# The opening of a diffusion layer kernel: modulation computed in four quarters instead of two halves

## The chip, the cores and the metric

The kernel runs on one core of one Trainium2 chip. The metric is the device time of one execution in microseconds (us). All arithmetic is in float32; large matrix products split each operand into a rounded part and a remainder and take three TensorE products.

## The reference, cut to what matters

One layer: adaLN-modulated RMSNorm, one wide input projection, two branches (attention and a gated MLP), an output projection, then a second modulated norm and an MLP. The change touches only what comes first:

```python
mod_x = jax.nn.silu(c) @ w_mod[l] + b_mod[l]            # c: 1024 values; w_mod: 1024 x 6144
sh1, sc1, g1, sh2, sc2, g2 = jnp.split(mod_x[:, None, :], N_MOD, axis=-1)
mod_c = jax.nn.silu(c_ctx) @ w_mod[l] + b_mod[l]        # the same for the context's vector
...
h_x = modulate(x, norm1_g[l], sh1, sc1)                 # rmsnorm(x, g) * (1 + scale) + shift
p_x = h_x @ w_in[l]                                     # x: 2048 tokens x 1024; w_in: 1024 x 3840
```

So the first projection needs the first two sixths of `w_mod` (shift and scale, 1024 columns each, 8 MB together) times two vectors, plus the first rows of `x`.

## The kernel before, in words

**Projection.** `project` treats 1024 tokens at a time as two blocks of 512 (`x0` and `x1` in the opening), and 1024 input channels as two halves of 512. Over this 2 x 2 split it uses a seven-product scheme: products 0, 1, 5, 6, 4, 2, 3 in this order (`SUMS`) replace eight. Product 0 needs only `x0`'s first 512 channels, product 1 only its second 512. Product 5 is the first that needs `x1`, through two differences per 128 channels (`h_five`). Each product runs in two chunks of 24 matmuls (`pairs_run`: four token tiles, two rows of 128 channels, three matmuls for the split operand, lines 1744 to 1746). Between chunks, and in the middle of one, `hook` runs a step of the generator `opening`.

**Operands.** `turn` transposes a 128-channel column of four token tiles on TensorE (line 192) and lets ScalarE apply scale and shift (line 537, from `G1` and `S1`). `operand` casts the result on ScalarE (line 572) and takes the remainder on VectorE (line 573). `pair_chunk` does the same for a weight chunk (lines 712, 713), and `opening_terms` builds weight differences for product 5 and on (lines 621 to 633; tiles `hx`, `f`). `leave` copies product 1's results out and `take` puts product 0's back (lines 2125, 727).

**Modulation.** `mod_head` loads `c`, `c_ctx`, `b_mod`, `norm1_g` and the spatial bias with five small transfers, loads `x0` and the weights for the first 512 channels (16 tiles of 128 x 512 from two places of `w_mod`), multiplies them (`mod_products`, line 339: 16 matmuls of 512 columns, 32 passes), and `mod_finish` turns the row into columns of `S1` and `G1` (lines 348 to 361). Then product 0 can start. The second half of the weights is loaded behind `x1`, and its 16 matmuls stand in `opening` after product 0. `h_scale` squares `x` on ScalarE (line 515), takes an inverse root on VectorE and multiplies `x` by it (line 524).

**Order.** The opening's instructions are pinned: each engine runs them in the order in which the code is written. All loads go through SyncE's queue in the written order. `at` in `pairs_run` sets how many weight chunks are prepared ahead.

Of the kernel before, what the change touches and what calls it, by code (L numbers as in the profile page):

```python
# [18 lines left out]
P = 128  # L19
# [48 lines left out]
CONTEXT_AT = 20  # L68
ON_VECTOR = (2, 4, 8, 14)
# [3 lines left out]
class Kern:  # L73
# [207 lines left out]
    def mod_head(self):  # L281
# [4 lines left out]
        at = 0  # L286
        for src, eng in (
            (I["c"][0], nc.sync),
            (I["c_ctx"], nc.sync),
            (I["b_mod"][0, : 2 * D], nc.scalar),  # L290
            (I["norm1_g"][0], nc.scalar),
        ):
            src = src.rearrange("(k p) -> k p", p=P)
            eng.dma_start(rows[at : at + src.shape[0]], src)
            at += src.shape[0]
        nc.scalar.dma_start(rows[at : at + GROUPS], I["gm_bs"][0])
        self.rope_consts()
        at += GROUPS
# [20 lines left out]
        w = self.mod_weights(0, "hx")  # L319
        self.h_scale(self.x0, dve=True)  # L320
        ps = self.bank([TB])
        for k in range(KC):
            self.mod_products(ps, w, k)
        self.mod_finish(ps, 0)

    def mod_weights(self, half, tag):
        w = []
        for k in range(KC):
            w.append([self.sb(tag, [TB]) for _ in range(2)])
            for i, t in enumerate(w[k]):  # L330
                lo = i * D + half * TB
                self.nc.sync.dma_start(
                    t, self.I["w_mod"][0, k * P : (k + 1) * P, lo : lo + TB]
                )
        return w

    def mod_products(self, ps, w, k):
        for i in range(2):
            self.nc.tensor.matmul(
                ps[32 * i : 32 * i + 32], self.wide[:, k, :], w[k][i],  # L340
                start=k == 0, stop=k == KC - 1,
            )

    def mod_finish(self, ps, half):
        nc = self.nc
        bcol, gcol = self.mod_cols
        row = self.t2([TB])
        nc.scalar.copy(row[:64], ps[:64])
        pt = self.bank([HK, 64])
        for j in range(HK):  # L350
            nc.tensor.transpose(
                pt[:, j, :], row[:64, j * P : (j + 1) * P], self.ident[:64, :64]
            )
        ks = slice(half * HK, (half + 1) * HK)
        for i, dst in enumerate((self.S1, self.G1)):
            bs = slice(i * KC + half * HK, i * KC + (half + 1) * HK)
            nc.vector.tensor_tensor(
                out=dst[:, ks], in0=pt[:, :, 32 * i : 32 * i + 2],
                in1=bcol[:, bs].unsqueeze(2).broadcast_to([P, HK, 2]), op=ALU.add,
            )  # L360
        nc.vector.scalar_tensor_tensor(
            out=self.G1[:, ks], in0=self.G1[:, ks], scalar=1.0,
            in1=gcol[:, ks].unsqueeze(2).broadcast_to([P, HK, 2]),
            op0=ALU.add, op1=ALU.mult,
        )
# [350 lines left out]
    def pairs_run(self, pairs, h, ready, hook, direct):  # L716
# [395 lines left out]
    def project(self, tail):  # L1112
# [4 lines left out]
        loaded = [self.pair_load(pairs[0], 0, c) for c in range(2)]  # L1117
        x1 = self.x_load(self.x_block(1), TT, lambda n: self.sb("hx", n), 2)
        wm = self.mod_weights(1, "h")
        loaded += [self.pair_load(pairs[0], 1, c) for c in range(2)]  # L1120
# [5 lines left out]
        h[0], h[1] = [], []  # L1126
        at = self.here()
        for kk in range(HK):
            t = raw[0, kk] = self.m4([2, TB])
            self.turn(self.x0, kk, t[:, 0])  # L1130
            if kk % 2 == 0:
                ready.append(self.pair_chunk(pairs[0], 0, kk // 2, loaded[kk // 2]))
            h[0].append(self.operand(0, t[:, 0]))
        self.h_scale(x1, dve=True)

        def opening(raw=raw, h=h):
            for _ in range(4):
                yield
            ps = self.bank([TB])
            for k in range(KC):  # L1140
                self.mod_products(ps, wm, k)
            self.mod_finish(ps, 1)
            for c in range(2):
                for kk in (2 * c, 2 * c + 1):
                    t = raw[0, kk]
                    self.turn(self.x0, kk + HK, t[:, 1])
                    h[1].append(self.operand(1, t[:, 1]))
                ready.append(self.pair_chunk(pairs[0], 1, c, loaded[2 + c]))
                next(terms)
# [13 lines left out]
            self.h_five(raw, h, 2)  # L1163
            next(terms)
            self.h_five(raw, h, 3)
            yield
            self.pins.append(range(at, self.here()))
            self.fences.append(range(at, self.here()))
            next(terms)
            yield  # L1170
            for _ in range(3):
                yield
                next(terms, None)
            for _ in range(CONTEXT_AT - 13):
                yield
# [1217 lines left out]
def kernel(ctx: ExitStack, tc: tile.TileContext, ins: dict, out: bass.AP):  # L2393
# [4 lines left out]
    "x", "c", "ctx", "c_ctx", "w_mod", "b_mod", "norm1_g", "norm2_g", "w_in", "q_norm_g",  # L2398
    "k_norm_g", "gm_norm_g", "gm_ws", "gm_bs", "w_br_attn", "w_br_gm", "w_out", "w_ff1",
# [35 lines left out]
```

## Time and profile before

| | |
|---|---|
| three runs | median 3011.93 us (3010.1 to 3013.86) |
| profiled execution | 3006.42 us, its span 3004.3 us |
| granted TensorE clock | 0.992 of full speed, mean |
| busy: TensorE / VectorE / ScalarE / GpSimd | 97% / 69% / 47% / 22% |
| VectorE busy in the span's first 116 us | 72.44 us |

The span runs from the first to the last instruction; the execution's own time is some 2 us longer. A row of the timeline gives start, duration, engine, line of the code, operation, output and inputs, shapes, and in brackets how long the engine sat idle before it and what ended that. "Windows" give the busy time of each engine in a stretch, then the granted clock (1.00 is full), the busy share of the DMA engines and what they moved.

### The profile page before, as it was taken

The numbers are of one execution on the slowest core, as the hardware profiler recorded it, in microseconds if no ns is written. First come the engines' busy times: TensorE is split into PE (matmuls) and PEld (weight loads), VectorE is DVE, ScalarE is ACT, GpSimd is POOL, SyncE is SP. The second block draws the span as 40 slices with busy tenths as digits, with TensorE's granted clock in tenths as the row PEclk, the third lists the DMA queues.
The fourth block names the chain that finished last, engine by engine and source line by source line (L and its number), as shares of the span: only waits on it lengthen the run. The fifth ranks groups of instructions, "written<-read, shape, count | busy, mean of one in ns | idle before, by whom it ended". The sixth has DMA issues, their size and how long they took to land.

```text
span 3004.3 us, 37936 instructions
## 1 busy us (share of the span) xinstructions
PE 2929.0 (97%) x13325; PEld 2211.2 (74%) x13325; DVE 2073.7 (69%) x2983; ACT 1418.8 (47%) x2318; POOL 654.0 (22%) x470
## 2 busy tenths in 40 slices
PE   7899999999999999999999989999999999999999
PEld 5778788876555555556888878888887888888887
DVE  4857487766888898777555588776676766654555
ACT  5645765554454454544222354444454344444432
POOL 0000000001999899894121200000000000000000
PEclk9999999999999999999999999999999999999999
DMA  7687966775010010016776659888766544447654
GB/s 269 190 288 258 313 211 215 255 250 163 24 36 29 22 37 22 22 43 193 232 218 188 189 194 320 306 302 306 262 218 221 182 152 155 154 164 267 210 210 154
DMA packets 386175, 559.04 MB, mean 186 GB/s; under 512 B 38640, under 2 KB 192416, under 8 KB 385984
## 3 DMA queue, kind: packets, MB, share of 16 engines
q1 hardware_dynamic: 373616, 535.89, 53.7%
q10 hardware_dynamic: 12368, 20.73, 1.8%
q8 instruction: 105, 1.72, 0.2%
q14 instruction: 86, 0.70, 0.1%
HBM read 379.75 MB, written 176.69 MB: 185 GB/s over the span
## 4 chain that ended last, share of the span: by engine, by line
PE 82%; DMA 7%; DVE 7%; ACT 2%; issue 2%; SPq 0%; POOL 0%; DVEq 0%; ACTq 0%; POOLq 0%
PE b L1744 14%; PE b L1745 14%; PE b L1746 14%; PE b L2322 9%; PE b L2291 5%; PE b L2310 4%; PE b L186 4%; PE b L187 4%; PE b L188 4%; PE b L2246 3%; PE a L1744 2%; PE a L1745 2%; PE a L1746 2%; PE b L192 1%; DMA m<-ws_d 1%
## 5 line engine op out<-in xcount | busy, mean ns | idle before, releaser
L2257 DVE TENSOR_REDUCE ts<-b 128x1 f32<-128x512 f32 x492 | 301.8, 681 | 66.9 <-PE b L2246 66.9
L2342 POOL TENSOR_TENSOR ac<-ac,p 128x512 f32<-128x512 f32 x214 | 313.6, 1498 | 48.3 <-ACT p L2314 48.3
L1860 DVE TENSOR_TENSOR b<-b,b 128x1024 fp32r<-128x1024 f32 x170 | 200.7, 1220 | 136.5 <-ACT b L1859 136.1
L1859 ACT CAST b<-b 128x1024 fp32r<-128x1024 f32 x170 | 170.7, 1051 | 226.1 <-PE b L1746 100.1
L2314 ACT ACTIVATE p<-b 128x512 f32<-128x512 f32 x384 | 193.8, 627 | 168.3 <-PE b L2310 160.6
L1745 PE MATMUL b<-b,b 128*128 128x512 f32 x680 | 265.1, 390 | 3.5 <-DVE b L1860 3.5
L1744 PE MATMUL b<-b,b 128*128 128x512 f32 x680 | 266.2, 391 | 2.3 <-DVE f L1881 1.4
L1746 PE MATMUL b<-b,b 128*128 128x512 f32 x680 | 264.7, 389 | 0.0
L2342 POOL TENSOR_TENSOR ac<-p,p 128x512 f32<-128x512 f32 x32 | 52.8, 1667 | 742.1 <-ACT p L2314 742.1
L2342 POOL TENSOR_TENSOR ac<-ac,t 128x512 f32<-128x512 f32 x152 | 198.9, 1337 | 0.0
L2291 PE MATMUL b<-h,h 128*128 128x512 f32 x576 | 187.0, 405 | 3.3 <-ACT p L2314 2.0
L2322 PE MATMUL b<-p,h 128*64 128x512 f32 x768 | 186.9, 610 | 0.0
L2310 PE MATMUL b<-h,h 128*128 128x512 f32 x576 | 178.6, 391 | 0.0
L1745 PE MATMUL b<-hb,b 128*128 128x512 f32 x446 | 173.8, 390 | 0.0
L1754 DVE TENSOR_TENSOR f<-f,b 128x512 f32<-128x512 f32 x160 | 109.1, 682 | 82.5 <-issue 47.8
L1744 PE MATMUL b<-hb,b 128*128 128x512 f32 x415 | 161.8, 390 | 0.0
L1746 PE MATMUL b<-hb,b 128*128 128x512 f32 x415 | 161.3, 389 | 0.0
L1745 PEld LDWEIGHTS b<-b,b 128*128 128x128 f32 x680 | 127.6, 188 | 31.7 <-DVE b L1860 5.0
L2291 PEld LDWEIGHTS b<-h,h 128*128 128x128 f32 x576 | 103.6, 188 | 63.9 <-DVE ts L2257 24.3
L1744 PEld LDWEIGHTS b<-b,b 128*128 128x128 f32 x680 | 127.7, 188 | 30.7 <-ACT b L1859 3.4
L1746 PEld LDWEIGHTS b<-b,b 128*128 128x128 f32 x680 | 127.6, 188 | 26.3
L1757 ACT ACTIVATE f<-f 128x512 f32<-128x512 f32 x96 | 60.5, 630 | 141.7 <-DVE f L1754 141.7
(440 smaller groups left out, 7260.8 us busy)
## 6 DMA issues: line engine op xcount, KB each, us to landing
ao_d<-f SPq DMA_DIRECT2D x224, 256.0 KB
f<-in_w_ff SPq DMA_DIRECT2D x48, 1024.0 KB
b<-ao_d SPq DMA_DIRECT2D x85, 512.0 KB
b<-w2o_d SPq DMA_DIRECT2D x85, 512.0 KB
w2o_d<-f SPq DMA_DIRECT2D x112, 256.0 KB
f<-in_w_in SPq DMA_DIRECT2D x38, 512.0 KB
f<-x_d SPq DMA_DIRECT2D x64, 256.0 KB
hb<-ao_d SPq DMA_DIRECT2D x54, 256.0 KB
```

Source lines behind the costliest of these rows:

```text
L186: mm(ps, sh, mh, start=start, stop=False)
L1744: mm(ps, wh, hh, start=start and k == 0, stop=False, skip_group_check=True)
L1745: mm(ps, wh, hl, start=False, stop=False, skip_group_check=True)
L1746: mm(ps, wl, hh, start=False, stop=k == len(w) - 1, skip_group_check=True)
L1859: nc.scalar.copy(h, f32(l))
L1860: nc.vector.tensor_tensor(out=l, in0=f32(l), in1=f32(h), op=ALU.subtract)
L2257: nc.vector.tensor_reduce(out=self.mx[:, t, h, c : c + 1], in_=ps[h], axis=AX.X, op=ALU.max)
L2291: self.nc.tensor.matmul(self.pts[j][h], k.KA[c][self.kv][:, ks], self.qa[h], start=True, stop=False, skip_group_check=True,)
L2310: self.nc.tensor.matmul(s, k.KB[c][self.kv][:, ks], self.qb[h], start=False, stop=True, skip_group_check=True,)
L2314: self.nc.scalar.activation(pt[h], s, AF.Exp)
L2322: nc.tensor.matmul(self.o[h * HD : (h + 1) * HD, :], k.V[c][:, i, self.kv * HD : (self.kv + 1) * HD], pt[h], start=j == 0, stop=j == NKT - 1,)
L2342: nc.gpsimd.tensor_tensor(out=self.acc[e][:, h], in0=old[:, h], in1=pt[h], op=ALU.add)
```

## The change

The weights of the modulation are laid out anew in HBM: `w_mod1[q, k]` holds, for quarter `q` (256 channels) and row block `k`, shift and scale columns side by side, so one transfer of 128 x 512 brings both. The five small vectors are concatenated to `head`, one transfer. The modulation runs in four quarters: quarter 0 in front of everything, quarters 1 to 3 in steps of `opening`. The row product of quarter 1 stands in the middle of product 0's first chunk, that of quarter 2 in the middle of its second; that of quarter 3 stands behind the whole first chunk of product 1. Each `quarter` prepares the operands of one chunk. `x1` is loaded behind the third quarter's weights, and it is scaled after quarter 2. The steps that turn `x1` and form product 5's operands come one or two steps later.

```diff
+MQ = 2
...
-        for src, eng in (
-            (I["c"][0], nc.sync),
-            (I["c_ctx"], nc.sync),
-            (I["b_mod"][0, : 2 * D], nc.scalar),
-            (I["norm1_g"][0], nc.scalar),
-        ):
...
+        at = I["head"].shape[0]
+        nc.sync.dma_start(rows[:at], I["head"])
         self.rope_consts()
...
+    def mod_weights(self, q, tag):
         w = []
         for k in range(KC):
+            t = self.sb(tag, [2, MQ * P])
+            self.nc.sync.dma_start(t.rearrange("p i c -> p (i c)"), self.I["w_mod1"][q, k])
+            w.append(t)
+        return w
+
+    def mod_row(self, w):
+        nc = self.nc
+        ps = self.bank([MQ * P])
+        for k in range(KC):
+            for i in range(2):
+                nc.tensor.matmul(
+                    ps[32 * i : 32 * i + 32], self.wide[:, k, :], w[k][:, i],
+                    start=k == 0, stop=k == KC - 1,
                 )
+        row = self.t2([MQ * P])
+        nc.scalar.copy(row[:64], ps[:64])
+        return row
...
-            depth = 3 if direct is None else min(3, max(1, at - 2))
+            depth = 3 if direct is None or at > 5 else 1
...
+        wm, loaded = [], []
+        for q in range(4):
+            if q == 3:
+                x1 = self.x_load(self.x_block(1), TT, lambda n: self.sb("hx", n), 2)
+            wm.append(self.mod_weights(q, "h" if q > 1 else "hx"))
+            loaded.append(self.pair_load(pairs[0], q // 2, q % 2))
...
+        def quarter(q, raw=raw, h=h):
+            j, c = q // 2, q % 2
+            for kk in (2 * c, 2 * c + 1):
+                if not j:
+                    raw[0, kk] = self.m4([2, TB])
+                t = raw[0, kk][:, j]
+                self.turn(self.x0, kk + j * HK, t)
+                if kk == 2 * c:
+                    ready.append(self.pair_chunk(pairs[0], j, c, loaded[q]))
+                h[j].append(self.operand(j, t))
+
+        quarter(0)
 
         def opening(raw=raw, h=h):
-            for _ in range(4):
-                yield
...
+            yield
+            row = self.mod_row(wm[1])
+            yield
+            self.mod_finish(row, 1)
+            quarter(1)
+            yield
+            row = self.mod_row(wm[2])
+            yield
+            self.mod_finish(row, 2)
+            quarter(2)
+            self.h_scale(x1, dve=True)
+            yield
+            yield
+            self.mod_finish(self.mod_row(wm[3]), 3)
+            quarter(3)
+            next(terms)
             yield
             turned = self.raw_turned(1, x1, raw, self.t4)
             next(turned)
             next(terms)
             yield
             next(turned)
+            next(terms)
             self.h_five(raw, h, 0)
+            self.h_five(raw, h, 1)
             yield
             next(turned)
-            self.h_five(raw, h, 1)
             next(terms)
+            self.h_five(raw, h, 2)
...
```

Line numbers move with the edit: line 537 becomes 524, 572 becomes 559, 524 becomes 511, 515 becomes 502, 348 becomes 330, 631 becomes 618, 2125 becomes 2124, 727 becomes 714, 1744 to 1746 become 1743 to 1745.

What the order of instructions shows, first on TensorE at product 0. Before, its four token tiles (`a_694` to `a_697`) run through and the second half of the modulation stands behind the whole product:

```order
L1746 MATMUL a_696<-f_99_634,h_649 128x384
L1744 MATMUL a_697<-f_99_634,h_637 128x384
L1745 MATMUL a_697<-f_43_515,h_637 128x384
L1746 MATMUL a_697<-f_99_634,h_638 128x384
L1744 MATMUL a_697<-f_99_634,h_648 128x384
L1745 MATMUL a_697<-f_43_515,h_648 128x384
L1746 MATMUL a_697<-f_99_634,h_649 128x384
L339 MATMUL b_754<-h_532,t_5_406 32x512
L339 MATMUL b_754<-h_533,t_5_406 32x512
```

After, on TensorE between the two pairs of token tiles of product 0's first chunk (`a_621` to `a_624`):

```order
L1745 MATMUL a_622<-f_90_603,h_618 128x384
L325 MATMUL b_637<-hx_466,t_5_402 32x256 x2
L325 MATMUL b_637<-hx_468,t_5_402 32x256 x2
L325 MATMUL b_637<-hx_470,t_5_402 32x256 x2
L325 MATMUL b_637<-hx_472,t_5_402 32x256 x2
L325 MATMUL b_637<-hx_474,t_5_402 32x256 x2
L325 MATMUL b_637<-hx_476,t_5_402 32x256 x2
L325 MATMUL b_637<-hx_478,t_5_402 32x256 x2
L325 MATMUL b_637<-hx_480,t_5_402 32x256 x2
L1743 MATMUL a_623<-f_90_603,h_606 128x384
```

A quarter's 16 matmuls of 256 columns moved into the chunk; the transposes of the next quarter follow the chunk.

Second, VectorE ahead of quarter 3 (`hx_516`, `hx_517` are parts of `x1`, `S_74` and `G_73` are `S1` and `G1`), after the change:

```order
L511 TENSOR_SCALAR hx_513<-hx_513,ts_798 128x512
L511 TENSOR_SCALAR hx_516<-hx_516,ts_798 128x512
L511 TENSOR_SCALAR hx_517<-hx_517,ts_798 128x512
L344 TENSOR_TENSOR S_74<-b_864,ts_405 128x4
L344 TENSOR_TENSOR G_73<-b_864,ts_405 128x4
L348 SCALAR_TENSOR_TENSOR G_73<-G_73,ts_406 128x4
L700 TENSOR_TENSOR f_68_538<-f_67_536,f_144_876 128x768
```

The scaling of `x1` stands ahead of quarter 3's columns; before, it stood ahead of the second half's.

Third, ScalarE from product 1's leaves to product 5's operands. Before (`t_148`, `t_153`: `x1` turned; `f_151`: product 5's weights; `h_894`: its first operand; `t_159`: a leave):

```order
L537 ACTIVATE t_148_847<-b_848,S_74,G_73 128x512
L537 ACTIVATE t_148_847<-b_854,S_74,G_73 128x512
L631 CAST f_151_860<-hx_806 128x384
L631 CAST f_151_860<-hx_833 128x384
L537 ACTIVATE t_153_878<-b_879,S_74,G_73 128x512
L537 ACTIVATE t_153_878<-b_885,S_74,G_73 128x512
L572 CAST h_894<-t_156_891 128x512
L2125 COPY t_159_904<-a_694 128x384
L2129 DMA p_d_0_129<-t_159_904 128x384
```

After (`t_161`: the second turned tile of `x1`; `t_160`: the last leave; `f_164`: product 5's weights; `h_976`, `h_983`: its first two operands):

```order
L2124 COPY t_160_950<-a_624 128x384
L2128 DMA p_d_0_129<-t_160_950 128x384
L714 COPY a_624<-t_116_702 128x384
L524 ACTIVATE t_161_954<-b_955,S_74,G_73 128x512
L524 ACTIVATE t_161_954<-b_961,S_74,G_73 128x512
L618 CAST f_164_967<-hx_895 128x384
L618 CAST f_164_967<-hx_932 128x384
L559 CAST h_976<-t_166_973 128x512
L559 CAST h_983<-t_169_980 128x512
```

The weights' cast and the first operands moved behind all four leaves of product 1 and behind the second turned tile. On VectorE at the same place, after the change:

```order
L620 TENSOR_TENSOR f_165_968<-hx_895,f_164_967 128x384
L620 TENSOR_TENSOR f_165_968<-hx_932,f_164_967 128x384
L570 TENSOR_TENSOR m_596<-m_596,t_154_917 128x512
L571 TENSOR_TENSOR t_166_973<-t_154_917,m_596 128x512
L560 TENSOR_TENSOR h_977<-t_166_973,h_976 128x512
L570 TENSOR_TENSOR m_610<-m_610,t_161_954 128x512
```

The remainder of the weights (line 620) stands ahead of the first operand's differences (570, 571), as before; the second operand's differences stand behind the first's remainder.

More of the change, by code (lines that the diff above doesn't have):

```diff
@@ L318, in mod_head, with mod_finish @@
         self.x0 = self.x_load(self.x_block(0), TT, self.t4)
-        w = self.mod_weights(0, "hx")
         self.h_scale(self.x0, dve=True)
[L321 to L326, printed above, removed]
+    def mod_weights(self, q, tag):
         w = []
         for k in range(KC):
[L329 to L333, printed above, removed]
-                )
[L335 to L344, printed above, removed]
+            t = self.sb(tag, [2, MQ * P])
[10 more added lines that the diff above has]
+                    start=k == 0, stop=k == KC - 1,
+                )
+        row = self.t2([MQ * P])
+        nc.scalar.copy(row[:64], ps[:64])
+        return row
+    def mod_finish(self, row, q):
         nc = self.nc
         bcol, gcol = self.mod_cols
[L347 to L350, printed above, removed]
+        pt = self.bank([MQ, 64])
+        for j in range(MQ):
             nc.tensor.transpose(
@@ L1116, in project @@
         at = self.here()
[L1117 to L1120, printed above, removed]
+        wm, loaded = [], []
[4 more added lines that the diff above has]
+            loaded.append(self.pair_load(pairs[0], q // 2, q % 2))
         raw, h = {}, [None] * 7
@@ L1126, in project @@
         h[0], h[1] = [], []
+        row = self.mod_row(wm[0])
+        self.mod_finish(row, 0)
         at = self.here()
[L1128 to L1134, printed above, removed]
-        def opening(raw=raw, h=h):
-            for _ in range(4):
-                yield
[L1139 to L1149, printed above, removed]
+        def quarter(q, raw=raw, h=h):
[9 more added lines that the diff above has]
+        quarter(0)
+        def opening(raw=raw, h=h):
+            yield
[14 more added lines that the diff above has]
+            next(terms)
             yield
```

32 lines of the change are left out of this document (15 added, 17 removed).

## The prediction

> **What bounds the kernel now.** The page comes first:
>
> ```profile
> span 3004.3 us, 37936 instructions
> PE 2929.0 (97%) x13325; PEld 2211.2 (74%) x13325; DVE 2073.7 (69%) x2983; ACT 1418.8 (47%) x2318; POOL 654.0 (22%) x470
> PE   7899999999999999999999989999999999999999
> ```
>
> TensorE is the bound; it idles 75 us of the span, and the first slice (75 us) is the emptiest. The change touches only this opening. So the question is how much later or earlier TensorE gets through it; behind it TensorE is nearly full, and a shift is carried to the end. The opening as the timeline has it (start, duration, engine, line):
>
> ```profile
> 11.87 11.12 PE L339 MATMUL b<-hx,t 128*32 128x512 f32 x32 [6.25 <-DMA hx<-in_w_mod]
> 23.02 0.58 ACT L348 COPY t<-b 64x512 f32<-64x512 f32 x1 [10.78 <-PE b L339]
> 23.66 0.46 PE L351 MATMUL b<-ident,t 64*128 64x64 f32 x4 [0.67 <-ACT t L348]
> 24.74 0.78 ACT L537 ACTIVATE m<-b,S,G 128x512 f32<-128x512 f32 x1 [1.14 <-PE b L192]
> 26.81 0.45 PE L1744 MATMUL a<-f,h 128*128 128x384 f32 x1 [0.80 <-ACT h L572]
> 27.47 0.62 ACT L572 CAST h<-m 128x512 fp32r<-128x512 f32 x1
> 31.27 0.52 PE L1744 MATMUL a<-f,h 128*128 128x384 f32 x1
> 38.12 7.06 PE L339 MATMUL b<-h,t 128*32 128x512 f32 x32
> 50.57 0.44 PE L1744 MATMUL a<-f,h 128*128 128x384 f32 x1 [2.27 <-ACT f L712]
> 58.97 0.42 PE L1744 MATMUL a<-f,h 128*128 128x384 f32 x1
> 61.14 1.04 PE L192 MATMUL b<-ident,hx 128*128 128x128 f32 x8
> 64.92 0.42 PE L1744 MATMUL a<-f,h 128*128 128x384 f32 x1
> 73.72 0.69 DVE L573 TENSOR_TENSOR h<-t,h 128x512 fp32r<-128x512 f32 x1 [0.68 <-ACT h L572]
> ```
>
> Row by row: the first half of the modulation waits for weights until 22.99; product 0 starts at 26.81, the second half of the modulation at 38.12, product 1 at 50.57, product 5 at 64.92; at 74.41 VectorE ends the last operand of product 5. From there to 94 VectorE has no idle time, and TensorE follows it. The windows (PE clock and DMA rate in the last columns) show two more things:
>
> ```profile
> 5.00:6.00 1.00, 0.31 (x1) 0.18 (x1) 0.00 (x0) 0.35 (x2) 0.00 (x0) 1.00 0.78 313
> 6.00:7.00 1.00, 0.00 (x0) 0.00 (x0) 0.00 (x0) 1.00 (x3) 0.00 (x0) 1.00 0.19 68
> 7.00:8.00 1.00, 0.00 (x0) 0.00 (x0) 0.00 (x0) 0.91 (x2) 0.00 (x0) 1.00 0.59 219
> 18.00:20.00 2.00, 2.00 (x8) 0.39 (x6) 0.00 (x0) 0.00 (x0) 0.00 (x0) 1.00 1.06 390
> 28.87:32.23 3.36, 3.36 (x10) 3.36 (x11) 2.25 (x3) 3.33 (x7) 0.00 (x0) 0.51 1.06 388
> 93.36:97.06 3.70, 3.70 (x12) 3.70 (x13) 3.48 (x6) 0.75 (x2) 0.00 (x0) 0.55 0.71 239
> ```
>
> First, the transfers have a hole: 313, 68 and 219 GB/s where 390 is the full rate, 570 KB or 1.5 us lost. Second, after a gap TensorE runs about 3.4 us at half clock (0.51, 0.55).
>
> **Front: time to the first product.** The hole's cause stands in SyncE's waits; each new transfer waits for an older one to land:
>
> ```profile
> SPq L332 <- DMA t<-in_x: 2.0, 1, 2.0
> SPq L332 <- DMA rg_k<-in_k_norm_g: 1.8, 1, 1.8
> SPq L332 <- DMA rg_q<-in_q_norm_g: 1.0, 1, 1.0
> ```
>
> With five small vectors in one transfer, four fewer stand before the weights, and the two gain rows go first on their queue; I take the hole as closed (-1.5; bound 0, if these waits only move). The first row product needs 8 weight tiles instead of 16, at 11.12/16 = 0.69 each: -5.5. Its last tile has half the columns: -0.4. It ends at 22.99 - 7.4 = 15.6. From its end to the first matmul were 3.8 (22.99 to 26.81); a copy and a set of transposes of half size take about 0.4 off. First matmul: 15.6 + 3.4 = 19.0, 7.8 us earlier than before. The extra instructions (two more finishes) cost VectorE and ScalarE about what the halves save, and lie inside the gaps counted next.
>
> **Quarters.** Twelve matmuls on fresh operands took 26.81 to 31.27, 4.5, because each waits for its cast and the clock falls to half; twelve on ready ones 2.2 (58.97 to 61.14). A row product of a quarter takes 7.06/2 = 3.5, its transposes come after the second twelve, and from there ScalarE's first scaled tile is 1.1 off (23.66 to 24.74) and the next matmul another 2.1 (24.74 to 26.81): 3.2. In these TensorE has 1.3 us of transposes and some 1.8 idle. Does that halve the clock? The nearest rows are these gaps, 2.05 (half clock behind it, above) and 0.94 (none, clock 1.00 in that window):
>
> ```profile
> 70.52 0.97 PE L1744 MATMUL a<-f,h 128*128 128x384 f32 x4 [0.94 <-ACT f L631]
> 92.36 0.95 DVE L713 TENSOR_TENSOR f<-f,f 128x768 fp32r<-128x768 f32 x1
> 93.36 0.45 PE L1745 MATMUL a<-f,h 128*128 128x384 f32 x1 [2.05 <-DVE f L713]
> ```
>
> 1.8 is nearer to 2.05, so I count it: 4.5 for the first twelve and 0.5 more for the row product (about 1.4 a quarter; bound 0). The Trainium skill, page "TensorE: Matmul & The Clock Gate", section "Part 1: The HAM clock gate", says that the clock halves after at least one idle window of about 3.4 us; by that, two quarters would lose 1.4 less each and the result would be 2.8 us lower. The 3.4 us of half clock agree with the row, the gap of 2.05 that brought them does not.
>
> - Quarter 0: 19.0 + 4.5 + 4.0 (row 1) + 2.2 + 3.2 = 32.9, first matmul of quarter 1.
> - Quarter 1: 32.9 + 4.5 + 4.0 (row 2) + 2.2 + 3.2 = 46.8, first of product 1.
> - Quarter 2: all 24 matmuls, 4.5 + 2.2, then row 3, 3.5: 57.0.
>
> Its follow-up would start quarter 3 at 57.0 + 3.4 = 60.4, but VectorE has x1's scaling in its queue ahead of that quarter's S1 and G1. The rows of that work:
>
> ```profile
> 31.25 0.62 ACT L515 ACTIVATE t<-hx 128x512 bf16<-128x512 f32 x1
> 36.29 0.16 DVE L517 TENSOR_TENSOR ts<-ts 128x4 f32<-128x4 f32 x1 [4.22 <-ACT t L515]
> 38.87 3.26 DVE L524 TENSOR_SCALAR hx<-hx,ts 128x512 f32<-128x512 f32 x8
> ```
>
> The squares start behind quarter 2's last cast, 1.3 after its first matmul (28.09 against 26.81): 48.1, take 5.0 (31.25 to 36.29), then VectorE 5.8 (36.29 to 42.13): 58.9. S1 and G1 0.5, scaled tile and casts 2.1: quarter 3 starts at 61.5, 1.1 of it due to x1. Before, product 1 began its first half at 50.57; the head start is gone.
>
> **Product 5, the term that decides.** From product 1's start to the end of x1's second transposes were 8.4 (50.57 to 58.97); the same work stands behind 61.5 now: 69.9. Before, product 5's operands were done a product earlier. Now ScalarE's queue has the leaves of product 1, then x1's second tiles, then the cast of product 5's weights, then the operands; VectorE has that weight's remainder ahead of the first difference. Their prices:
>
> ```profile
> 56.90 0.91 ACT L631 CAST f<-hx 128x384 fp32r<-128x384 f32 x2
> 57.42 1.03 DVE L633 TENSOR_TENSOR f<-hx,f 128x384 fp32r<-128x384 f32 x2 [1.46 <-ACT f L631]
> 58.37 0.68 DVE L583 TENSOR_TENSOR m<-m,t 128x512 f32<-128x512 f32 x1
> 58.82 1.45 ACT L537 ACTIVATE t<-b,S,G 128x512 f32<-128x512 f32 x2 [1.01 <-PE b L192]
> 59.09 0.69 DVE L584 TENSOR_TENSOR t<-t,m 128x512 f32<-128x512 f32 x1
> 60.16 0.61 ACT L572 CAST h<-t 128x512 fp32r<-128x512 f32 x1
> ```
>
> Tiles 1.45, cast 0.9, remainder 0.65 behind it, two differences 1.4, cast 0.6: 5.0, and product 5 starts at 74.9, not at 64.92. Its second operand (remainder 0.7, differences 1.4, cast 0.6, remainder 0.7) is whole at 78.3; six more matmuls 1.1, x1's third transposes 1.0, tiles 1.45: 81.9. The third operand's differences and cast (2.0) give 83.9, the last tiles 1.45, cast of the second weights 0.9, remainder 0.65, differences 1.4, cast 0.6, remainder 0.7: 89.6. Before, that was 74.41: **15.2 us later**. VectorE's list from there to product 4's weights (74.41 to 93.31, no idle) holds the same work, so TensorE gets them at 108.5. TensorE's gap there falls under 1 us, since its own products 6 and 4 start late too, and the half clock behind 93.36 (1.6) goes. The net shift is 15.2 - 1.6 = 13.6.
>
> What follows hangs on product 4's end: the reload for product 3 stands behind its stores on SyncE, and the stall after it moves along:
>
> ```profile
> 99.79 0.55 DVE L2127 TENSOR_TENSOR t<-t,a 128x384 f32<-128x384 f32 x1
> 101.21 1.05 SPq L710 DMA_DIRECT2D f<-t_d  x1
> PE b L999 <- ACT m L528: 6.0, 2, 5.5
> ```
>
> Everything later is the same work in the same order. **Sum:** 3006.4 (the profiled execution's own time) + 13.6 = 3020.0. The median shown, 3011.9, lies 5.5 above that execution; on its scale 3025.5, say 3026.
>
> **Rivals.**
> 1. Faster: the head start is kept, because ScalarE and VectorE stay ahead of TensorE throughout, as they do in the middle of product 1 now. Then TensorE's own work is the bound: from 19.0 six halves of 4.4, three row products of 3.5, three sets of transposes of 1.3 and four of 1.04 end product 5 at 64.0, and its last operand comes by 62, 12 before the 74.41 of now; of this I would count the 7.8 of the front as surely kept: 3004. It decides where product 5's last operand is whole: before 68 the kernel is faster by over 6. Against it: both queues are strictly in the order quoted, with the cast behind the tiles and the remainder ahead of the differences.
> 2. No difference: the waits come as said, but smaller by half (quarters warm -2.8, transfers faster, product 3's stall absorbs some, as two gate weights now go ahead of product 4's last store): about +5, 3017; with more luck within 6 us. Against: the reload still stands behind that store.
> 3. The front doesn't do what it says: the hole stays: +1.5, 3027.
> 4. More half clock: product 5's waits (5.0 and 3.4) bring another 1.6 or two: 3029.
>
> **Chances.** What a measurement of this kernel can tell from no change is 0.2%, 6 us. The forecast with rivals 3 and 4: 0.70 (0.50, 0.08, 0.12), slower. Rival 2: 0.17, of which I put almost all within 6 us of before. Rival 1: 0.13. The forecast's own range is 3018 to 3033 (bounds of clock, hole, waits). To 8 in 10: the low end reaches into rival 2, 3009, and the high end stays at 3033; outside lie rival 1 and a little of either end.
>
> **What would show it.** First product matmul near 19 and full DMA rate from 4 us: front right. Gaps of about 1.8 before each quarter, clock under 0.8 around them: quarters right. TensorE waiting for ScalarE's h at product 5 for about 5 us, VectorE's list ending 13 to 15 later than 99.8: the deciding term right. It is wrong if product 5 starts before 68, or if the shift at product 4 isn't the shift at the end.

## Result and profile after

The changed kernel takes 3035.48 us (median of 4 runs, 3034.5 to 3039.47) where the kernel before takes 3012.89 on the same chip (4 runs, 3010.1 to 3014.46): ratio 1.0078, 95% interval 1.0061 to 1.0096. It is slower by 22.6 us; forecast were 13.6 (3026, range 3009 to 3033). The direction is right, the time is outside the range. One of the six runs of e3 further down took 3194.4 us at a granted clock of 0.872 instead of 0.99 and is left out of that kernel's median.

The page after: the same saturated TensorE, and a first slice (76 us) that went from 7 tenths busy to 6, a second from 8 to 7.

```profile
span 3033.3 us, 38065 instructions
PE 2938.8 (97%) x13389; PEld 2218.1 (73%) x13389; DVE 2077.9 (69%) x2989; ACT 1419.9 (47%) x2320; POOL 653.0 (22%) x470
PE   6799999999999999999999989999999999999999
```

The timeline of the opening after (start, duration, engine, line), the rows that answer to those of before:

```profile
12.31 5.81 PE L325 MATMUL b<-hx,t 128*32 128x256 f32 x32 [8.94 <-DMA hx<-in_w_mod]
21.60 0.44 PE L1743 MATMUL a<-f,h 128*128 128x384 f32 x1 [1.67 <-ACT h L559]
35.47 0.44 PE L1743 MATMUL a<-f,h 128*128 128x384 f32 x1 [1.67 <-ACT h L559]
49.24 0.44 PE L1743 MATMUL a<-f,h 128*128 128x384 f32 x1 [1.67 <-ACT h L559]
58.05 3.25 DVE L511 TENSOR_SCALAR hx<-hx,ts 128x512 f32<-128x512 f32 x8
61.22 0.15 DVE L344 TENSOR_TENSOR S<-b,ts 128x4 f32<-128x4 f32 x1
64.11 0.44 PE L1743 MATMUL a<-f,h 128*128 128x384 f32 x1 [2.43 <-ACT h L559]
78.64 0.69 PE L1743 MATMUL a<-f,h 128*128 128x384 f32 x1 [6.33 <-ACT h L559]
93.25 0.69 DVE L560 TENSOR_TENSOR h<-t,h 128x512 fp32r<-128x512 f32 x1 [0.68 <-ACT h L559]
```

The first product starts at 21.60 (before 26.81), the next quarters at 35.47, 49.24 and 64.11, and product 5 at 78.64. The last row is product 5's last operand, begun at 73.72 before and at 93.25 now: 19.5 us later. That row is the yardstick for all runs below.

The windows (PE clock and DMA rate in the last columns). The weak stretch at the head is not gone but moved: 98, 165 and 232 GB/s from 3 to 6 us, where the kernel before has 299, 410 and 313 there and its weak stretch from 6 to 8. And at product 5 the clock is half:

```profile
3.00:4.00 1.00, 0.31 (x1) 0.18 (x1) 0.00 (x0) 0.18 (x1) 0.00 (x0) 1.00 0.45 98
4.00:5.00 1.00, 0.00 (x0) 0.00 (x0) 0.03 (x1) 0.00 (x0) 0.00 (x0) 1.00 0.73 165
5.00:6.00 1.00, 0.00 (x0) 0.00 (x0) 0.76 (x7) 0.00 (x0) 0.00 (x0) 1.00 0.71 232
36.00:40.00 4.00, 3.79 (x11) 2.71 (x11) 1.19 (x2) 1.20 (x3) 0.00 (x0) 0.65 1.05 386
76.00:84.00 8.00, 4.07 (x11) 3.23 (x12) 6.50 (x12) 1.24 (x2) 0.00 (x0) 0.50 0.07 27
```

ScalarE's own timeline ahead of product 5 shows what the prediction had not priced:

```profile
72.42 0.47 ACT L2124 COPY t<-a 128x384 f32<-128x384 f32 x1
73.29 0.48 ACT L714 COPY a<-t 128x384 f32<-128x384 f32 x1 [0.40 <-ACT t L2124]
73.71 1.44 ACT L524 ACTIVATE t<-b,S,G 128x512 f32<-128x512 f32 x2
75.05 0.92 ACT L618 CAST f<-hx 128x384 fp32r<-128x384 f32 x2
77.97 0.62 ACT L559 CAST h<-t 128x512 fp32r<-128x512 f32 x1 [2.01 <-DVE t L571]
```

x1's second transposes end at 72.31 on TensorE (71.28 and 1.03), but their scaled tiles begin at 73.71, behind the copies of product 1's last leave. (A leave is the copy that takes product 1's result out, line 2124, together with the copy that puts product 0's back, line 714.)

### The profile page after: what moved, and what is told of

Same layout as the page of the kernel before. It is cut to its first block, busy times and chain, and to the rows that moved or that the text cites. A ratio compares the mean times of both kernels' runs of the same rounds, so it can differ in the third digit from the quotient of the medians.

```text
span 3033.3 us, 38065 instructions
## 1 busy us (share of the span) xinstructions
PE 2938.8 (97%) x13389; PEld 2218.1 (73%) x13389; DVE 2077.9 (69%) x2989; ACT 1419.9 (47%) x2320; POOL 653.0 (22%) x470
## 5 line engine op out<-in xcount | busy, mean ns | idle before, releaser
L1743 PE MATMUL a<-f,h 128*128 128x384 f32 (+1 forms) x320 | 121.5, 384 | 23.0 <-ACT h L559 18.1
```

The costliest lines, as they stand in the source:

```text
L1743: mm(ps, wh, hh, start=start and k == 0, stop=False, skip_group_check=True)
```

## Experiments

All runs in one table. "Operand" is the start of the last operand of product 5 on VectorE, beside 73.72 in the first profile of before; the times are medians, beside that of before on the same chip. The row is not the same in every execution: the kernel before itself has 72.08 in its second profile (e0), so against that one every "later by" is 1.6 more. And the first product's start, 21.60 in the changed kernel, lies between 21.02 and 22.00 in e2, e3, e4 and e6, which change nothing ahead of it.

| run | operand | later by | time | before there | ratio (95%) |
|---|---|---|---|---|---|
| changed kernel | 93.25 | 19.5 | 3035.5 | 3012.9 | 1.0078 (1.0061 to 1.0096) |
| e1_gains_late | 113.29 | 39.6 | 3054.2 | 3013.2 | 1.0136 (1.0119 to 1.0154) |
| e2_five_early | 88.82 | 15.1 | 3030.0 | 3013.2 | 1.0062 (1.0049 to 1.0074) |
| e3_x1_ahead | 83.70 | 10.0 | 3029.8 | 3013.2 | 1.0059 (1.0042 to 1.0075) |
| e6_fillers | 92.90 | 19.2 | 3031.5 | 3013.2 | 1.0066 (1.0051 to 1.0080) |
| e0_before_again | 72.08 | -1.6 | 3010.9 (one run) | 3009.0 | |
| e7_gains_behind | 90.55 | 16.8 | 3032.6 | 3009.0 | 1.0079 (1.0064 to 1.0094) |
| e4_second_half_whole | 76.11 | 2.4 | 3015.9 | 3009.0 | 1.0019 (1.0007 to 1.0031) |
| e8_before_front | 69.87 | -3.9 | 3007.9 | 3009.0 | 0.9996 (0.9984 to 1.0008) |
| e9_front_filled | 68.55 | -5.2 | 3011.5 | 3011.0 | 1.0002 (0.9993 to 1.0012) |
| e10_mended | 78.45 | 4.7 | 3022.2 | 3011.0 | 1.0038 (1.0025 to 1.0050) |

**e1, the gain rows later on ScalarE's queue.** These two loads are issued by ScalarE; SyncE's queue has the loads of `x`, of `head` and of the weights.

```diff
         nc.sync.dma_start(rows[:at], I["head"])
-        self.rope_consts()
...
         quarter(0)
+        self.rope_consts()
```

> The changed kernel with the two gain rows (rg_q, rg_k) loaded behind quarter 0 instead of at the start. Theory: their 256 short packets at the head of the transfers keep the front slow (98 to 232 GB/s from 3 to 6 us), and this is what was missed in the front; the first product matmul moves from 21.6 to about 19, the whole kernel by -2.6 us against the changed kernel (some 3033). Rival: the transfers start slowly whatever goes first (the rows of x themselves): first matmul at 21.6 as before, no change in time.

The front came to 19.03, so the rows of the gains are what holds it up. But the kernel lost another 20 us. From the timeline, ScalarE's two DMA issues and the copy behind them, then TensorE's next work:

```profile
46.56 0.39 ACTq L441 DMA_DIRECT2D rg_q<-in_q_norm_g  x1
47.52 0.36 ACT L329 COPY t<-b 64x256 f32<-64x256 f32 x1 [27.21 <-DMA h<-in_w_in]
47.94 0.47 PE L337 MATMUL b<-ident,t 64*128 64x64 f32 x2 [18.07 <-ACT t L329]
```

Written behind all loads of the opening, these two issues waited, by the profile, for one of those loads to land, 27.2 us, and everything behind them in ScalarE's queue waited too. The issue itself costs 0.4 us; its place cost TensorE 18.

**e7, the gain rows on SyncE's queue, behind the opening's loads,** and their scaling on VectorE behind product 5's last operand (the expectation says behind quarter 3).

```diff
-        self.rope_consts()
...
             loaded.append(self.pair_load(pairs[0], q // 2, q % 2))
+        self.gain_rows()
...
             self.h_five(raw, h, 3)
+            self.gain_scale()
```

> The changed kernel with the two gain rows loaded on SyncE's queue behind all loads of the opening (and scaled on VectorE behind quarter 3). Theory (the rows' short packets at the head of the queues cost the front 2.6 us, and in the first experiment ScalarE's queue stood still because the issue of these loads there waited for an older transfer): first product matmul at 19.0, no long wait of ScalarE, all quarters 2.6 earlier, opening 15.4 later than before (18.0 in the changed kernel), time 3033 where the changed kernel has 3035.5. Rival: the front is earlier, but VectorE's and ScalarE's lists at product 5 end no earlier, since the weights of quarters 2 and 3 set them: first matmul 19.0, opening still 17 to 18 later.

Windows and timeline of this run:

```profile
3.00:4.00 1.00, 0.00 (x0) 0.00 (x0) 0.65 (x6) 0.18 (x1) 0.00 (x0) 1.00 0.84 315
4.00:5.00 1.00, 0.00 (x0) 0.00 (x0) 0.05 (x1) 0.04 (x1) 0.00 (x0) 1.00 1.00 410
5.00:6.00 1.00, 0.00 (x0) 0.00 (x0) 0.00 (x0) 1.00 (x2) 0.00 (x0) 1.00 1.05 426
9.61 5.85 PE L324 MATMUL b<-hx,t 128*32 128x256 f32 x32 [6.62 <-DMA hx<-in_w_mod]
18.94 0.44 PE L1746 MATMUL a<-f,h 128*128 128x384 f32 x1 [1.67 <-ACT h L560]
```

The rate is full from 4 us, the row product ends at 15.46 (predicted 15.6) and the first product starts at 18.94 (predicted 19.0). The 2.7 us reach the operand row (16.8 against 19.5): the theory of the front holds. In the time they can't be seen (1.0079 against 1.0078); the intervals are 3 permille wide, 9 us.

**e2, product 5's weights and first operand one step earlier.**

```diff
             quarter(3)
             next(terms)
+            next(terms)
+            next(terms)
             yield
             turned = self.raw_turned(1, x1, raw, self.t4)
             next(turned)
+            self.h_five(raw, h, 0)
             next(terms)
             yield
             next(turned)
+            self.h_five(raw, h, 1)
             next(terms)
-            self.h_five(raw, h, 0)
-            self.h_five(raw, h, 1)
...
```

> The changed kernel with product 5's weight cast and first operand one step earlier: behind quarter 3 all of the first differences and the cast, then each turned tile of x1 followed at once by its operand. Theory (product 5's late operands decide the opening): its first matmul from 78.6 to about 76, its last operand from 93.9 to about 90, time -3 to -4 against the changed kernel (some 3032). Rival (the waits at product 5 are absorbed by VectorE's list behind it): TensorE waits less there, the same time within 1 us.

**e3, x1 loaded ahead of quarter 2's weights, scaled in two parts** (squares and root behind quarter 1, scaling behind quarter 2), its tiles and product 5's operands right behind quarter 3.

```diff
-            if q == 3:
+            if q == 2:
                 x1 = self.x_load(self.x_block(1), TT, lambda n: self.sb("hx", n), 2)
...
             quarter(1)
+            root = self.h_root(x1)
...
             quarter(2)
-            self.h_scale(x1, dve=True)
+            self.h_apply(x1, root, True)
+            next(terms)
+            next(terms)
...
             quarter(3)
-            next(terms)
-            yield
             turned = self.raw_turned(1, x1, raw, self.t4)
             next(turned)
             next(terms)
-            yield
             next(turned)
-            next(terms)
             self.h_five(raw, h, 0)
...
```

> The changed kernel with x1 loaded ahead of quarter 2's weights, its squares behind quarter 1, its scaling behind quarter 2, and its first two columns turned right behind quarter 3, with product 5's first operands behind them. Theory: quarter 3 starts about 1 us earlier, product 5's first matmul at about 71 instead of 78.6, its last operand at about 84 instead of 93.9, time -9 to -10 against the changed kernel (some 3026), so the late second rows were nearly half of the loss. Rival (absorbed later): under -4.

Product 5's first two waits in the timeline, of e2 and then of e3:

```profile
72.78 0.62 PE L1743 MATMUL a<-f,h 128*128 128x384 f32 x1 [2.13 <-ACT h L559]
78.24 0.69 PE L1743 MATMUL a<-f,h 128*128 128x384 f32 x1 [4.05 <-ACT h L559]
```

```profile
72.14 0.44 PE L1750 MATMUL a<-f,h 128*128 128x384 f32 x1 [2.71 <-ACT a L720]
77.61 0.69 PE L1750 MATMUL a<-f,h 128*128 128x384 f32 x1 [1.85 <-ACT a L720]
```

The operand row comes 4.4 us (e2) and 9.5 (e3) earlier than in the changed kernel. Of this 0.6 and 0.5 stand already at the first product (21.02 and 21.11 against 21.60), so order alone is worth about 4 and 9. In e2 product 5 starts 5.9 earlier. In e3 it waits for ScalarE's copies at the leaves (line 720 puts product 0's result back) instead of the operands' casts. The times, 1.0062 and 1.0059, lie below the 1.0078, but their intervals (up to 1.0074 and 1.0075) overlap that of the changed kernel (from 1.0061). The rows end where they were expected (89.5 and 84.4, about 90 and 84 expected); of the times, e2's 3030.0 is under the 3032 expected, e3's 3029.8 over the 3026.

**e4, only the first half in quarters;** the second half whole, x1 loaded ahead of quarter 2's weights and scaled behind quarter 1, the steps after that as before.

```diff
-            if q == 3:
+            if q == 2:
                 x1 = self.x_load(self.x_block(1), TT, lambda n: self.sb("hx", n), 2)
...
             quarter(1)
+            self.h_scale(x1, dve=True)
             yield
-            row = self.mod_row(wm[2])
             yield
-            self.mod_finish(row, 2)
+            rows = [self.mod_row(wm[2]), self.mod_row(wm[3])]
+            self.mod_finish(rows[0], 2)
+            self.mod_finish(rows[1], 3)
             quarter(2)
-            self.h_scale(x1, dve=True)
-            yield
-            yield
-            self.mod_finish(self.mod_row(wm[3]), 3)
+            next(terms)
             quarter(3)
...
```

> The changed kernel with its first half in two quarters and its second half whole: rows 2 and 3 in one go behind product 0, then both their finishes; x1 loaded ahead of their weights and scaled behind quarter 1; steps behind that as in the kernel before. Theory (quarters 2 and 3 with their waits, x1's scaling in the wrong place and product 5's operands late cost the opening, not the front): quarter 1 starts at 35.5, rows 2 and 3 end near 50, product 1 starts at 52 to 53.5 where before has 50.57 and the changed kernel 49.24; product 5 follows as in before, its last operand at 76 to 78; opening 2 to 4 later than before instead of 18, time 3015 to 3018. Rival (the loads laid out in quarters or the finer finishes cost by themselves): product 5's first matmul still waits over 4 us, opening later by 8 or more, time over 3021.

Its timeline at product 1, at product 5's start and in product 5's second half:

```profile
53.71 0.45 PE L1742 MATMUL a<-f,h 128*128 128x384 f32 x1 [0.80 <-ACT h L559]
66.80 0.42 PE L1742 MATMUL a<-f,h 128*128 128x384 f32 x1
72.90 0.97 PE L1742 MATMUL a<-f,h 128*128 128x384 f32 x4 [0.94 <-ACT f L618]
76.13 0.44 PE L1742 MATMUL a<-f,h 128*128 128x384 f32 x1 [0.76 <-ACT h L559]
```

Product 5 starts at 66.80 without a wait, where the changed kernel waits 6.33 and then 1.28 in its first half; the waits of 0.94 and 0.76 in the second half are those of before (1.50 and 0.66 in the changed kernel). Product 1 starts 4.5 later than in the changed kernel, and yet the last operand comes 17.1 earlier. So 17.1 of the 19.5 belong to the second half in quarters with the order that stands around it, and the time follows: 1.0019 instead of 1.0078, the intervals well apart. What of it is the splitting and what the order e4 doesn't separate; e3 has some 9 from order alone. The layout of the weights and the finer finishes are in e4 too, which is 2.4 later in all.

**e6, TensorE kept busy** in the gaps of quarters 1 to 3 by four extra 128x512 matmuls that no output reads.

```diff
                 h[j].append(self.operand(j, t))
+                if q and kk % 2:
+                    ps = self.bank([TB])
+                    for _ in range(4):
+                        self.nc.tensor.matmul(
+                            ps, self.ident, self.x0[0][0][:, :TB], start=True, stop=True
+                        )
```

> The changed kernel with four more matmuls (128 x 512, into a bank that nothing reads) in the gap before each of quarters 1 to 3; work added, nothing left out. Theory (the gaps of 1.7 us halve the clock behind them, about 1.4 us each): clock near 1.00 behind quarters 1 to 3, time -3 to -4 against the changed kernel (some 3032). Rival (the clock falls whatever stands in the gap, or the first matmuls' waits hide it): clock as before, time the same or up to +1 each by the fillers themselves.

Windows, and the extra matmuls of quarter 1 and the row behind it in the timeline:

```profile
28.00:36.00 8.00, 8.00 (x51) 5.27 (x48) 1.13 (x4) 2.64 (x5) 0.00 (x0) 1.00 1.06 386
36.00:40.00 4.00, 4.00 (x20) 2.76 (x20) 1.51 (x3) 1.84 (x4) 0.00 (x0) 1.00 1.05 386
76.00:84.00 8.00, 5.33 (x16) 4.39 (x17) 5.41 (x9) 1.23 (x2) 0.00 (x0) 0.50 0.23 84
33.97 3.60 PE L1133 MATMUL b<-t,ident 128*128 128x512 f32 x8
39.58 2.78 PE L325 MATMUL b<-h,t 128*32 128x256 f32 x24
```

The clock stays full at 36 to 40 where the changed kernel has 0.65. The four cost 3.6 us, more than the gap, and row 2 still starts at 39.58 instead of 40.07. At product 5 little is left of it (92.90 against 93.25): there ScalarE and VectorE set the end. The median, 3031.5, is what the theory said, but the row gives it no such gain, and the interval overlaps that of the changed kernel: the agreement in the time may be luck.

**e0, the kernel before once more.** No edit.

> The kernel before, unchanged, profiled a second time. Question: the opening of the changed kernel is 18.0 us later (at 168 us), its end 28.7 us later in the two profiles, 22.6 by the medians. Theory (the profile of before was a run of the quick end, 3006.4 where the median is 3013): a second profile stands within 1 us of the first up to 170 us and is 2 to 8 us later at the end, and gets later at the same places, between 200 and 770 us and between 1860 and 2080 us. Rival (the change itself makes the later work slower): the second profile stays within 2 us of the first at those places, or gets later at others.

The same gap ahead of product 4, then the clock behind it, in this second profile; below, the clock at the same place in the first:

```profile
91.74 0.44 PE L1745 MATMUL a<-f,h 128*128 128x384 f32 x1 [2.04 <-DVE f L713]
92.00:94.00 2.00, 2.00 (x13) 2.00 (x13) 2.00 (x4) 0.49 (x1) 0.00 (x0) 1.00 0.88 296
94.00:96.00 2.00, 2.00 (x13) 2.00 (x12) 2.00 (x5) 1.05 (x2) 0.00 (x0) 1.00 0.55 174
```

```profile
94.00:96.00 2.00, 2.00 (x8) 2.00 (x7) 2.00 (x4) 0.11 (x1) 0.00 (x0) 0.50 0.76 249
```

A gap of 2.05 halved the clock in one execution; a gap of 2.04 at the same place didn't in the other. The first profile also lost 1.6 us behind the first product, the second nothing, and product 1 starts at 48.97 instead of 50.57. By the start of the same matmul in both, counted from the last, the second profile is 3.7 ahead of the first at 168 us and 4.5 behind at the end. So neither theory was right as written: the opening is not the same within 1 us, and most of the later loss comes between 750 and 770 us (5.2 of 8.2), the rest in smaller steps. One profile places a difference at the end no better than to 5 us or so.

**e8, the kernel before with the front alone:** five vectors in one transfer, gain rows behind the loads.

```diff
-        at = 0
-        for src, eng in (
...
-        self.rope_consts()
+        at = I["head"].shape[0]
+        nc.sync.dma_start(rows[:at], I["head"])
...
         loaded += [self.pair_load(pairs[0], 1, c) for c in range(2)]
+        self.gain_rows()
```

> The kernel before with only the front of the change and of e7: five small vectors in one transfer, gain rows loaded behind the opening's loads. Theory (the hole of 1.5 us and the short packets are taken out of the way of the weights): no window under 380 GB/s between 5 and 20 us, first product matmul at 24.5 to 25.3 where before has 26.81, and the shift is carried to product 5: opening 1.5 to 2.3 earlier, time 3011. Rival: the second row's weights or the product's operands set the second half, so the first matmul is earlier and the rest is not: opening within 0.5 of before, time 3013.

**e9, e8 with extra matmuls** in two gaps (`fill(n)`: n matmuls as in e6, no output reads them).

```diff
             h[0].append(self.operand(0, t[:, 0]))
+            if kk == HK - 1:
+                self.fill(1)
...
                     h[1].append(self.operand(1, t[:, 1]))
+                if c:
+                    self.fill(2)
```

> The kernel before with the front of e8 (one transfer for the small vectors, gain rows behind the opening's loads) and extra 128x512 matmuls into an unread bank in two gaps of TensorE: one (about 0.9 us) behind the last turned tile of product 0's first half, two behind that of its second half, ahead of product 1. They are left-over work that no output reads. Theory (the clock halves behind such gaps in some executions): the clock stays 1.00 from 24 to 60 us, product 0's second row starts at 34.3 to 35.0 where e8 has 35.88, and at 93 us it is 5 earlier than before where e8 is 3.8; time 1 to 2 under e8's. Rival (product 3 waits for the reload of what product 4 stored, and that wait takes what came earlier: 5.5 us in before, 7.2 in e8): at 168 us no more than 3.5 earlier, time that of e8, within 0.1% of before.

The first product of e8 in the timeline and its clock in a window; then the clock of e9 and, of the waits from 100 to 170 us, the one ahead of product 3 in e9 and in the second profile of before:

```profile
24.60 0.44 PE L1737 MATMUL a<-f,h 128*128 128x384 f32 x1 [0.80 <-ACT h L563]
28.00:40.00 12.00, 12.00 (x59) 8.82 (x59) 6.96 (x24) 7.71 (x22) 0.00 (x0) 0.89 1.03 371
```

```profile
28.00:40.00 12.00, 12.00 (x65) 7.84 (x65) 7.04 (x24) 7.74 (x23) 0.00 (x0) 1.00 1.06 380
80.00:100.00 20.00, 18.08 (x101) 17.19 (x100) 18.91 (x42) 11.31 (x21) 0.00 (x0) 1.00 0.65 203
PE b L990 <- ACT m L519: 6.9, 2, 6.4
```

```profile
PE b L999 <- ACT m L528: 7.9, 2, 7.3
```

Both openings do what was expected: first product at 24.60 (2.2 earlier than 26.81), the clock full to 100 us in e9, operands 3.9 and 5.2 earlier than in the first profile of before, 2.2 and 3.5 earlier than in the second. The times don't follow: 0.9996 and 1.0002. The wait ahead of product 3 doesn't show why: it is 7.2 in e8 and 6.4 in e9, but 5.5 and 7.3 in the two profiles of the kernel before. And the rival's other sign failed, for by the same matmul e9 is still 8.1 ahead of the first profile at 168 us and 4.5 ahead of the second. Where the gain goes stays open. Neither beats the kernel before by what can be told here. e9's profile is that of its shortest run, 2997.4 of a median of 3011.5, so its opening is not a proof for the rest.

**e10, all mends together:** e3 with e7's gain rows and two extra matmuls in each quarter's gap.

> The changed kernel with everything that helped put together: x1 loaded ahead of quarter 2's weights and scaled in two parts, its tiles and product 5's operands made right behind quarter 3 (e3), gain rows behind the loads (e7), and two extra matmuls that no output reads behind the turns of each quarter (half of e6's). Theory (the parts add up, and what stays is the work of four halves one behind the other: quarters of 13 us against 24 for a whole half): first product matmul at 19.0 to 19.9, product 5's first matmul at 68 to 70 (72.14 in e3, 73.74 in before for its second half at the latest), 7 to 9 later than before at 93 us, time 7 to 10 over before. Rival A (ScalarE and VectorE set the end of the opening, so an earlier front is lost there): 10 to 11 later at 93 us as in e3. Rival B (the quarters do as well as before once these are mended): within 3 of before at 93 us, time the same.

The clock behind quarter 1 and product 5's first two waits:

```profile
28.00:36.00 8.00, 7.70 (x39) 4.64 (x39) 2.65 (x6) 6.35 (x16) 0.00 (x0) 1.00 1.06 385
66.91 0.44 PE L1760 MATMUL a<-f,h 128*128 128x384 f32 x1 [2.40 <-ACT a L721]
72.37 0.44 PE L1760 MATMUL a<-f,h 128*128 128x384 f32 x1 [2.82 <-ACT a L721]
```

Product 5 starts at 66.91, earlier than expected, and the last operand is 4.7 later than before: the parts more than add up at the row (10.0 of e3 less the 2.7 of e7 and the 0.3 of e6 would be 7.0). The time doesn't show it, 11.2 over before where 7 to 10 were expected. What remains is slower than before, 1.0038, and its row is 9.9 behind that of e9, which has the same front and the two halves whole. Product 5 still waits for the copies at the leaves (2.40 and 2.82), so how much of the 9.9 another order would take off is not shown.

## Why the prediction was right and wrong

- **Hole in the transfers: wrong.** The step "the two gain rows go first on their queue; I take the hole as closed" is the one that failed. Their transfers (32 KB each, in packets of 256 bytes) now run beside the first loads: 98, 165 and 232 GB/s against 315, 410 and 426 once they are out of the way (e7). Cost: 2.6, since the first product started at 21.60, not 19.0. Two runs show the cause, e7 with 18.94 and e1 with 19.03. They show it at the row; the time of e7 is that of the changed kernel. The row product's own terms were right: e7 ends it at 15.46 and starts at 18.94.
- **Quarters: right.** 13.9 each were predicted, 13.87 and 13.77 measured, with the gap (1.67) and the half clock. Quarter 3's start was 42.5 behind the first product as predicted (64.11 - 21.60 = 42.51), x1's scaling ending right ahead of S1.
- **Product 5: mechanism right, size short by 1.7.** It waited for ScalarE's operand, 6.33 where 5.0 were forecast, 1.3 more. The copies of product 1's leaves, which the prediction named but gave no price, stand ahead of x1's tiles and make them 1.4 late (73.71 behind 72.31). From there the last operand came 0.6 later than reckoned, and 0.2 had been gained ahead of it (8.2 instead of 8.4 from quarter 3 to the end of the transposes). e2 and e3 show the cause by their runs: the same work in another order takes about 4 and 9 off. e4, which also leaves the second half whole, takes 17.1 off.
- **Half clock behind product 4 (-1.6): a property of one execution, not of the kernel.** In the changed kernel the gap there is under 1 us, as the prediction said, and the clock is full behind it (1.00 from 104 to 128):

```profile
113.54 0.45 PE L1744 MATMUL a<-f,h 128*128 128x384 f32 x1 [0.53 <-DVE f L700]
```

  Before, the same matmul started at 93.36 behind 2.05 of idle time. So against the first profile of before the shift, by the start of the same matmul, falls there from 20.2 to 18.6, and is 18.0 at 168 us. But e0 has the gap without the half clock, and against it the shift stays at 21.8. The prediction counted the term as the kernel's own. The changed kernel also had new half clock at product 5 (0.50 from 76 to 84), so rival 4 came true in part; what it cost is within the 0.6 above.
- **Sum.** For the operand row 15.2 were forecast, and 15.2 + 2.6 + 1.7 = 19.5. For the time 13.6 were forecast and the medians say 22.6, 9.0 more: 2.6 and 1.7; the 1.6 behind product 4; and 1.6 that the first profile of before had lost behind its first product and e0 had not (its operand row is 21.2 ahead of that of the changed kernel). The last two hold if e0 is the more usual of the two executions, which two profiles can't tell. Another 1.0 of the miss of 10 is the median of before, 3012.9 on that chip instead of 3011.9. The remaining 1.5 stay open: over the ten kernels of the table that were timed against before, the time is between 1 under and 7 over the shift of the operand row, and on average 4 over (2 over, counted from the row of e0). The prediction's own sign, that the shift at product 4 is the shift at the end, did not hold between the two profiles: 18.0 at 168 us and 28.7 at the end (21.6 and 24.1 against e0). One place behind the opening can be named, and it differs between two executions of the kernel before itself: by the same matmuls, e0, the changed kernel and five of the experiments lose 4.9 to 6.4 us on the first profile between 750 and 772 us of its time; e2, e3, e6 and e9 lose nothing there.
- **Rivals.** Rival 1 needed product 5's last operand before 68; it began at 93.25. Even with every mend it stays at 78.45 (e10). What it took for granted, that a gain at this row is carried to the end, isn't borne out either: e8 and e9 have the row 3.9 and 5.2 earlier and the time of before. Rival 2 is refuted by the time. Rival 3 came true with more than its price.

The range was too narrow by the same failing: the bounds of the hole (0 to 1.5) left out that it could grow, and nothing was added for what executions of one kernel differ by.

## What to carry to other kernels

When a step is cut into quarters, write down each engine's queue in order and price everything between the producer and the operand, copies and leaves included: the head start of 5 us was real, and it was lost several times over some 55 us later, where about 9 us went by the order of the work alone. Move a small transfer by where it stands among the queue's older ones, not by when it is needed; the same two loads cost 2.7 us at the head, 18 on ScalarE's queue behind the other loads, and nothing to be seen on SyncE's behind the rest. A shift of a few us in the opening is shown by a row of the trace, not by the time, if two runs of one kernel differ by more; and the row, too, moved by 1.6 between two profiles of one kernel.

## What was not expected of the hardware

- **The same gap halves the clock in one execution and not in the other.** Gaps of 2.05 and 2.04 us at the same place: half clock in one execution, full in the other. The Trainium skill, page "TensorE: Matmul & The Clock Gate", section "Part 1: The HAM clock gate", says that the activity window runs freely and isn't aligned with the kernel, so that the cold stretch at a kernel's start varies from run to run; the two profiles show the same in the middle of a kernel. In each trace of this case the stretches of half clock start on one grid of 3.41 us (in the changed kernel at 23.56, 37.21, 50.87, 64.52 and 74.76: steps of four, four, four and three times 3.41). On that grid the gap of the first profile (91.31 to 93.36) lies whole in one stretch, and that of the second (89.70 to 91.74) is cut in two at 91.26. The stretch with the gap in the first profile, then the one with its larger part in the second:

```profile
90.35:93.77 3.42, 1.37 (x8) 1.05 (x7) 3.42 (x6) 2.46 (x5) 0.00 (x0) 1.00 0.75 232
87.85:91.26 3.41, 1.85 (x11) 1.53 (x9) 3.41 (x6) 1.84 (x4) 0.00 (x0) 1.00 0.45 144
```

  TensorE was busy for 1.37 us of the one, and half clock followed; for 1.85 of the other, and it didn't. Over all such stretches of the twelve traces, half clock followed all 90 at full clock in which TensorE was busy for less than 0.44 of the time, 30 of 52 between 0.44 and 0.55, and 13 of some 10,200 above. That is a count, not a rule that was put to the test. That a whole idle window of 3.4 us must pass, as the same section of the Trainium skill has it, is not what the traces show: gaps of 1.67 with some transposes before them were followed by 0.65 in the window from 36 to 40, and by 1.00 when the gap was filled (e6).
- **Two small loads more than halve the rate of the big ones.** 64 KB in short packets (256 bytes) took about 0.7 MB off what was moved from 3 to 6 us (0.50 MB against 1.15 in e7).
- **A DMA issue can hold a compute engine.** ScalarE stood 27.2 us, by the profile, for a transfer that was none of its own (e1).
